# Output projections of a two-layer encoder: one matmul of 512 columns for both halves of the activations

## The chip, the cores and the metric

The kernel runs on one core of one Trainium2 chip. The metric is the device time of one execution in microseconds (us); lower is better. Engines are named as the profile names them: PE is TensorE's matmuls and PEld its weight loads, DVE is VectorE, ACT is ScalarE, POOL is GpSimd, SP is SyncE, which here issues the weight loads from DRAM. ACTq rows are DMAs that ScalarE issues.

## What is computed

The reference is an encoder of 2 layers on 256 tokens of 1024 features, in float32. Each layer is a feed-forward half step, a token mixer, and a second feed-forward half step, all added to the residual x:

```python
x = x + 0.5 * swiglu(rms_norm(x, norm_ffn1[l]), ffn1_in[l], ffn1_out[l])
h = rms_norm(x, norm_mix[l])
proj = h @ w_in[l]
p_rwkv, p_attn, p_gate = jnp.split(proj, [C_RWKV, C_RWKV + C_ATTN], axis=-1)
...
y = jnp.einsum('bsgc,gcd->bsgd', branches, w_branch[l])
merged = jnp.sum(gates * y, axis=2)
x = x + merged @ w_out[l]
x = x + 0.5 * swiglu(rms_norm(x, norm_ffn2[l]), ffn2_in[l], ffn2_out[l])
```

`swiglu` multiplies by a weight matrix of 1024 x 5632 on the way in and by one of 2816 x 1024 on the way out. The mixer runs a bidirectional RWKV-7 scan (branch A) and a differential attention (branch B) side by side; `w_out` is 1024 x 1024.

## The kernel before

Activations lie feature-major: features in the 128 partitions, then the feature tile, then the 256 tokens. Weights stream from DRAM once, in pieces of 128 x 1024 (`weights`, L129 to L140): SP loads `wr`, ACT rounds it to float32r as `wh` (L135), DVE subtracts to get the low part `wl` (L139). `wr` and `wh` have 3 buffers each, `wl` has 2. Activations are split in the same way into a high and a low part. A product of two split operands is three matmuls (`mm3`, L142 to L147): high weights by high part, high weights by low part, low weights by high part. Each has a stationary operand of 128 x 128 and 256 moving columns, the tokens, and all add into one PSUM accumulator `acc`, of which there are 3, each a bank of 512 float32 per partition.

A feed-forward half (`ffn`, L186 to L216) first makes 22 tiles of hidden features, then 8 tiles of output: for each output tile 22 groups of three matmuls, of which the hidden tiles' parts are the moving operands (`hh` and `hl`, six slots shared with mixer tiles and printed in the profile under those names: ar, wt, ab, qb). The tile is added to x by one DVE instruction (L215), and `x_ready` (L150 to L166) at once makes the parts for the next stage: the high part on ACT (L158), the low part on DVE (L159), the square on ACT (L165), its sum over the tiles on POOL (L166). `rstd` (L168 to L183) turns that sum into the norm's factor for every token: a PE matmul (L172), DVE (L174), a power on POOL (L176), DVE (L179), a PE matmul (L181) and a copy on ACT into `rs` (L183). The stage that follows scales its results by `rs` on draining, so its matmuls start earlier than `rs` is there.

The mixer (`mix`, L805 to L840) stores x to DRAM (`xd`, L809), computes lambda from four small vectors that it loads (`lambdas`, L613 to L627: the load at L617, a product and a sum on DVE at L620 and L621, an exponential on ACT at L622), projects, scans and attends in the order of a written plan, and ends with the branch projection (`branch`, L734 to L745, merged at L825 to L828), the load of x back from `xd` (L833) and the output projection (L834 to L840), 8 tiles of 8 groups of three matmuls, again with one addition a tile (L839). Gate tiles (`gates`, L722 to L732: a projection, a DVE scaling at L729, a tanh on ACT at L730) are independent work in it. The attention's own projections (L643 to L645) have the weights as the moving operand, 512 columns of float32r.

Each engine runs its instructions in the order of the program. Within a stage a scheduler in the framework fixes that order when the kernel is built, from priorities and its own timeline; the plan, pool sizes and priorities are the same in both kernels.

Of the kernel before, what the change touches and what calls it, by code (L numbers as in the profile page):

```python
# [54 lines left out]
class Trunk:  # L55
# [21 lines left out]
    def slot(self, tag, shape, dt=F32, half=False):  # L77
        """A tile of 8 KB (or 4) in a partition; tiles of one tag follow each other in place."""
        tag, n = PLACE.get(tag, tag), int(np.prod(shape[1:]))
        t = self.sp.tile([P, 1024 if half else 2048], dt, tag=tag, name=self.nm(tag))  # L80
        v = t[:, :n]
        names = "abcd"[:len(shape) - 1]
        if len(names) > 1:
            v = v.rearrange(f"p ({' '.join(names)}) -> p {' '.join(names)}", **dict(zip(names, shape[1:])))
        return v
# [42 lines left out]
    # weights ------------------------------------------------------------------------------------  # L128
# [13 lines left out]
    def mm3(self, out, w, c, xh, xl, first, last):  # L142
        wh, wl = w[0][:, c * P:(c + 1) * P], w[1][:, c * P:(c + 1) * P]
        mm = self.nc.tensor.matmul
        mm(out, wh, xh, start=first, stop=False)  # L145
        mm(out, wh, xl, start=False, stop=False)  # L146
        mm(out, wl, xh, start=False, stop=last)  # L147

    # the residual and its norm ------------------------------------------------------------------
    def x_ready(self, l, g0, k, start, later=0):  # L150
        """Splits gain * x of one feature tile and adds its squares."""
        nc = self.nc
        x, g = self.x[:, k], self.vec[l][:, g0 + k:g0 + k + 1]
        if start:
            self.xh = self.slot("xh", [P, KD, S], F32R)
            self.xl = self.slot("xl", [P, KD, S], F32R)
# [28 lines left out]
    # feed-forward half step ---------------------------------------------------------------------  # L185
    def ffn(self, l, w_in, w_out, nxt):  # L186
        nc = self.nc
        xh, xl = self.xh, self.xl
        self.rstd()
        hh = [self.slot(f"b{i}", [P, 8, S], F32R) for i in range(3)]  # L190
        hl = [self.slot(f"b{i + 3}", [P, 8, S], F32R) for i in range(3)]
        for j in range(KF):
            ps = self.acc()
            for u in range(2):
                w = self.weights(w_in[j, :, u * 1024:(u + 1) * 1024], 1024)
                for k in range(KD):
                    self.mm3(ps[:, u * S:(u + 1) * S], w, k, xh[:, k], xl[:, k], k == 0, k == KD - 1)
# [7 lines left out]
            a, b = hh[j // 8][:, j % 8], hl[j // 8][:, j % 8]  # L205
            nc.scalar.activation(a, h, AF.Copy)
            nc.vector.tensor_tensor(b, h, a.bitcast(F32), ALU.subtract)
        for j in range(KD):
            ps = self.acc()
            for c in range(3):  # L210
                n = min(8, KF - 8 * c)
                w = self.weights(w_out[j, :, c * 1024:c * 1024 + n * P], n * P)
                for k in range(n):
                    self.mm3(ps[:, :S], w, k, hh[c][:, k], hl[c][:, k], c + k == 0, c == 2 and k == n - 1)
            nc.vector.scalar_tensor_tensor(self.x[:, j], ps[:, :S], 0.5, self.x[:, j], ALU.mult, ALU.add)  # L215
            nxt(j)  # L216

    # one tile of x @ W for two feature tiles, in a bank -----------------------------------------
    def project(self, w_in, tiles):
        ps = self.acc()  # L220
        for i, t in enumerate(tiles):
            w = self.weights(w_in[t], 1024)
            for k in range(KD):
                self.mm3(ps[:, i * S:(i + 1) * S], w, k, self.xh[:, k], self.xl[:, k], k == 0, k == KD - 1)
        return ps

    def shifted(self, l, tiles, outs):
        """outs = p + mu * (centred_shift(p) - p) of RWKV column tiles."""
# [25 lines left out]
    # RWKV-7: everything that the scans need -----------------------------------------------------  # L254
    def rwkv_common(self, l):
        """The low-rank parts and the places of what the pairs of heads give."""
# [58 lines left out]
    def rwkv_pair(self, p):  # L315
        """A pair of heads in both directions; the last part of the second direction waits for the next call."""
# [16 lines left out]
    def turn(self, out, a):  # L333
        """out[h] = a[h].T for both halves of the partitions."""
# [25 lines left out]
    def unit_front(self, p, d, st, sig, a2, da):  # L360
# [3 lines left out]
        # 2 * iclr - 1 = tanh of half the logit  # L364
# [32 lines left out]
    def unit_back(self, p, d, st, bw, kw):  # L397
# [26 lines left out]
        if d == 1:  # L424
            # sum over a head of r * r_k * (k of both directions)
# [8 lines left out]
    # (I - A)^-1 of the 32 x 32 diagonal blocks, one in a partition ---------------------------------  # L434
    def invert(self, q):
# [25 lines left out]
        # 16 x 16 blocks, row by row from below: X[i, j:] = G[i, j:] X[j:, j:]  # L461
# [7 lines left out]
        # the block off the diagonal: X01 = X00 G01 X11, with X00 G01 in the place below G's diagonal  # L469
# [19 lines left out]
    def merge_blocks(self, q):  # L489
        """The blocks off the diagonal: T = D + D A D."""  # L490
# [118 lines left out]
    # differential attention -----------------------------------------------------------------------  # L609
# [56 lines left out]
    def attention_core(self, l):  # L666
# [3 lines left out]
        for h in range(4):  # L670
# [17 lines left out]
            # e0 / s0 - lambda * e1 / s1 = (e0 - lambda * s0 / s1 * e1) / s0  # L688
# [32 lines left out]
    # the token mixer ------------------------------------------------------------------------------  # L721
# [199 lines left out]
```

## Time and profile before

| what | value |
|---|---|
| median of 3 runs | 1410.98 us (1410.39 to 1412.33) |
| profiled execution, first to last instruction (span) | 1406.5 us |
| time of the profiled execution around its span | not given by the profile; the median stands 4.5 us above the span |
| mean granted TensorE clock | 0.987 of full speed |
| PE, PEld busy | 1349.9 us (96%), 1285.0 us (91%) |
| DVE, ACT, POOL busy | 940.7 us (67%), 664.8 us (47%), 288.2 us (20%) |
| first feed-forward's additions to x | from 150.93 to 206.61 us |

The stages follow each other in the span: feed-forward, mixer and feed-forward of the first layer, then the same of the second. Matmuls are pipelined: a row's duration is its latency, and the distance from one start to the next is what it takes of the engine. "Idle before" an instruction tells how long its engine waited and for whom.

### The profile page before, as it was taken

To read this page: it belongs to the slowest core of one execution; us is meant where nothing else is said; L and a number is where in the kernel's file an instruction comes from. 1 tells how busy PE (TensorE), PEld (TensorE's weight loads), DVE (VectorE), ACT (ScalarE), POOL (GpSimd) and SP (SyncE) were. 2 spreads that over 40 slices of the span, in tenths; PEclk is the share of its full clock that TensorE was granted. 3 is DMA by queue.
4 is the path that set the end of the run, shared out by engine and by line. 5 is a ranking of instruction groups with operands and counts; after the bars stand their busy time and mean duration, and the time that the engine had idled before them with its cause. 6 is when DMAs were issued, how large, how long until landed. Compare 5 with 4: busy or idle time off the path is not lost.

```text
span 1406.5 us, 30996 instructions
## 1 busy us (share of the span) xinstructions
PE 1349.9 (96%) x12916; PEld 1285.0 (91%) x12916; DVE 940.7 (67%) x1421; ACT 664.8 (47%) x1059; POOL 288.2 (20%) x284
## 2 busy tenths in 40 slices
PE   6999999998989999999999999999988999999999
PEld 6999998877889899999999999988767888999998
DVE  4655557799957766555556655588999577656644
ACT  5444445344444455444444444554543554544432
POOL 3111015445001112111111111154540010211100
PEclk9999999999999999999999999999999999999999
DMA  6555664325333565556655556633352445555564
GB/s 230 182 181 182 180 207 156 99 91 138 108 103 116 191 229 177 185 181 179 181 184 187 183 174 183 218 111 113 93 143 83 114 136 193 175 187 184 183 188 143
DMA packets 90333, 227.60 MB, mean 162 GB/s; under 512 B 29264, under 2 KB 35408, under 8 KB 89680
## 3 DMA queue, kind: packets, MB, share of 16 engines
q1 hardware_dynamic: 78640, 207.16, 47.0%
q10 hardware_dynamic: 11552, 18.46, 3.9%
q8 instruction: 101, 1.65, 0.5%
q14 instruction: 40, 0.33, 0.1%
HBM read 214.05 MB, written 11.53 MB: 160 GB/s over the span
## 4 chain that ended last, share of the span: by engine, by line
PE 80%; DVE 11%; DMA 3%; issue 2%; ACT 2%; POOL 2%; ACTq 0%; SPq 0%; DVEq 0%; POOLq 0%
PE acc L147 23%; PE acc L146 23%; PE acc L145 23%; DVE tv L458 3%; DVE wl L139 3%; DVE lora L459 2%; PE back L331 1%; PE gen L331 1%; PE att L679 1%; PE back L337 1%; PE gen L283 1%; DMA x<-xd 1%; DMA x<-x 1%; DMA f<-g 0%; PE acc L643 0%
## 5 line engine op out<-in xcount | busy, mean ns | idle before, releaser
L135 ACT ACTIVATE wh<-wr 128x1024 fp32r<-128x1024 f32 (+1 forms) x390 | 404.9, 1039 | 414.7 <-PE acc L146 268.6
L139 DVE TENSOR_TENSOR wl<-wr,wh 128x1024 fp32r<-128x1024 f32 (+1 forms) x390 | 475.5, 1219 | 171.0 <-PE acc L147 83.0
L145 PE MATMUL acc<-xh,wh 128*128 128x256 f32 x1904 | 540.2, 286 | 11.8 <-ACT wh L135 11.8
L146 PE MATMUL acc<-xl,wh 128*128 128x256 f32 x1904 | 539.5, 285 | 0.0
L147 PE MATMUL acc<-xh,wl 128*128 128x256 f32 x1904 | 529.9, 286 | 2.4 <-DVE wl L139 2.1
L145 PEld LDWEIGHTS acc<-xh,wh 128*128 128x128 f32 x1904 | 367.0, 193 | 17.3 <-ACT wh L135 12.0
L146 PEld LDWEIGHTS acc<-xl,wh 128*128 128x128 f32 x1904 | 367.0, 193 | 3.2 <-issue 2.5
L147 PEld LDWEIGHTS acc<-xh,wl 128*128 128x128 f32 x1904 | 360.6, 193 | 9.4 <-issue 3.5
L204 POOL TENSOR_TENSOR t<-t,t 128x256 f32<-128x256 f32 x88 | 89.3, 1016 | 403.7 <-ACT t L202 403.7
L145 PE MATMUL acc<-ar,wh 128*128 128x256 f32 x512 | 144.9, 283 | 0.0
L147 PE MATMUL acc<-ar,wl 128*128 128x256 f32 x512 | 144.9, 283 | 0.0
L199 DVE TENSOR_TENSOR t<-acc,rs 128x512 f32<-128x512 f32 x88 | 60.8, 692 | 119.7 <-PE acc L147 114.6
L146 PE MATMUL acc<-wt,wh 128*128 128x256 f32 x384 | 108.9, 284 | 0.0
L145 PEld LDWEIGHTS acc<-ar,wh 128*128 128x128 f32 x512 | 98.3, 192 | 0.0
L147 PEld LDWEIGHTS acc<-ar,wl 128*128 128x128 f32 x512 | 98.3, 192 | 0.0
L145 PE MATMUL acc<-wt,wh 128*128 128x256 f32 x320 | 91.0, 286 | 3.4 <-DVE x L839 2.2
L166 POOL TENSOR_TENSOR vv<-vv,t 128x256 f32<-128x256 f32 x42 | 36.8, 876 | 279.4 <-ACT t L165 271.8
L147 PE MATMUL acc<-wt,wl 128*128 128x256 f32 x320 | 91.5, 286 | 1.3 <-DVE wl L139 1.2
L458 DVE TENSOR_TENSOR tv<-lora 64x8 f32<-64x8 f32 (+10 forms) x88 | 74.9, 852 | 1.9
L146 PEld LDWEIGHTS acc<-wt,wh 128*128 128x128 f32 x384 | 74.4, 194 | 0.0
L146 PE MATMUL acc<-ab,wh 128*128 128x256 f32 x256 | 72.4, 283 | 0.0
L145 PEld LDWEIGHTS acc<-wt,wh 128*128 128x128 f32 x320 | 61.9, 194 | 4.0 <-issue 2.4
(234 smaller groups left out, 1935.1 us busy)
## 6 DMA issues: line engine op xcount, KB each, us to landing
wr<-f1i SPq DMA_DIRECT2D x88, 512.0 KB, 3.7
wr<-f2i SPq DMA_DIRECT2D x88, 512.0 KB, 3.6
wr<-win SPq DMA_DIRECT2D x62, 512.0 KB, 3.6
wr<-f1o SPq DMA_DIRECT2D x32, 512.0 KB, 3.6
wr<-f2o SPq DMA_DIRECT2D x32, 512.0 KB, 3.6
wr<-watt SPq DMA_DIRECT2D x24, 512.0 KB, 3.7
wr<-wbr SPq DMA_DIRECT2D x16, 512.0 KB, 3.6
wr<-wout SPq DMA_DIRECT2D x16, 512.0 KB, 3.4
```

Of the source, the lines that this page charges most:

```text
L135: nc.scalar.activation(wh[:, :n], raw[:, :n], AF.Copy)
L139: nc.vector.tensor_tensor(wl[:, :n], raw[:, :n], wh[:, :n].bitcast(F32), ALU.subtract)
L145: mm(out, wh, xh, start=first, stop=False)
L146: mm(out, wh, xl, start=False, stop=False)
L147: mm(out, wl, xh, start=False, stop=last)
L166: nc.gpsimd.tensor_tensor(self.sq, self.sq, sq, ALU.add)
L199: nc.vector.tensor_tensor(gu, ps.rearrange("p (a b) -> p a b", a=2), self.rs.unsqueeze(1).to_broadcast([P, 2, S]), ALU.mult)
L204: nc.gpsimd.tensor_tensor(h, s, gu[:, 1], ALU.mult)
L283: mm(ps, dw[r, t * P:(t + 1) * P], w2[r], start=True, stop=True)
L331: self.nc.tensor.matmul(out[r], a[r], b[r], start=start, stop=stop)
L458: mul = lambda o, a, b: ops.append(nc.vector.tensor_tensor(o, a, b, ALU.mult).ins)
L459: add = lambda o, a: ops.append(nc.vector.tensor_reduce(o, a, AX.X, ALU.add).ins)
```

## The change

The high and low part of an activation now lie in one tile, so that both can be read as one moving operand of two pieces of 256 columns. In the output projections of both feed-forward halves and of the mixer, `mm3` gives way to `mmw`: one matmul of 512 columns by the high weights, which fills both halves of the accumulator, and one of 256 columns by the low weights into the left half. The two halves are added on draining: `add_x` has two additions in place of one. `mm3` stays for all other products and only takes its operands from the common tile.

```diff
-    def mm3(self, out, w, c, xh, xl, first, last):
+    def mm3(self, out, w, c, x, first, last):
         wh, wl = w[0][:, c * P:(c + 1) * P], w[1][:, c * P:(c + 1) * P]
         mm = self.nc.tensor.matmul
...
+    def mmw(self, out, w, c, x, first, last):
+
+        wh, wl = w[0][:, c * P:(c + 1) * P], w[1][:, c * P:(c + 1) * P]
+        mm = self.nc.tensor.matmul
+        mm(out.rearrange("p (a b) -> p a b", a=2), wh, x, start=first, stop=last, skip_group_check=True)
+        mm(out[:, :S], wl, x[:, 0], start=False, stop=last, skip_group_check=True)
+
+    def add_x(self, j, ps):
+        for u in range(2):
+            self.nc.vector.scalar_tensor_tensor(self.x[:, j], ps[:, u * S:(u + 1) * S], 0.5, self.x[:, j], ALU.mult, ALU.add)
...
-            self.xh = self.slot("xh", [P, KD, S], F32R)
-            self.xl = self.slot("xl", [P, KD, S], F32R)
+            self.xs = self.sp.tile([P, 2, KD, S], F32R, tag="xs", name=self.nm("xs"))
+            self.xh, self.xl = self.xs[:, 0], self.xs[:, 1]
...
-        hh = [self.slot(f"b{i}", [P, 8, S], F32R) for i in range(3)]
-        hl = [self.slot(f"b{i + 3}", [P, 8, S], F32R) for i in range(3)]
+        hs = [self.slot(f"b{i}", [P, 2, 4, S], F32R) for i in range(6)]
...
-                    self.mm3(ps[:, :S], w, k, hh[c][:, k], hl[c][:, k], c + k == 0, c == 2 and k == n - 1)
-            nc.vector.scalar_tensor_tensor(self.x[:, j], ps[:, :S], 0.5, self.x[:, j], ALU.mult, ALU.add)
+                    self.mmw(ps, w, k, hs[2 * c + k // 4][:, :, k % 4], c + k == 0, c == 2 and k == n - 1)
+            self.add_x(j, ps)
...
-        mh, ml = self.slot("wt0", [P, KD, S], F32R), self.slot("wt1", [P, KD, S], F32R)
+        ms = [self.slot(f"wt{i}", [P, 2, 4, S], F32R) for i in range(2)]
...
-                self.mm3(ps[:, :S], w, k, mh[:, k], ml[:, k], k == 0, k == KD - 1)
-            nc.vector.scalar_tensor_tensor(self.x[:, j], ps[:, :S], 0.5, self.x[:, j], ALU.mult, ALU.add)
+                self.mmw(ps, w, k, ms[k // 4][:, :, k % 4], k == 0, k == KD - 1)
+            self.add_x(j, ps)
```

New lines push the later ones down by 10 or 11: L159 becomes L170, L174 L185, L233 L243, L620 L630, and so on. The order of the instructions moves at places that the diff does not show, since the scheduler lays them anew.

TensorE at the end of the first feed-forward's output projection and the start of the mixer (`acc` of the last output tile, then that of the mixer's first), before:

```order
L145 MATMUL acc_2327<-wt_20_167,wh_2390 128x256
L146 MATMUL acc_2327<-qb_170,wh_2390 128x256
L147 MATMUL acc_2327<-wt_20_167,wl_2392 128x256
L147 MATMUL acc_2459<-xh_1775,wl_2464 128x256
L145 MATMUL acc_2459<-xh_1775,wh_2462 128x256
```

and with the change:

```order
L153 MATMUL acc_2178<-qb_169,wh_2225 128x512
L154 MATMUL acc_2178<-qb_169,wl_2227 128x256
L153 MATMUL acc_2178<-qb_169,wh_2225 128x512
L154 MATMUL acc_2178<-qb_169,wl_2227 128x256
L145 MATMUL acc_2289<-xs_1753,wh_2292 128x256
```

A group of three has become a group of two. VectorE at the same place and in the front of the first mixer (`x` is the residual, `xl` and `xs` its parts, `wl` low weights, `lam` lambda, `rs` the norm's factor), before:

```order
L215 SCALAR_TENSOR_TENSOR x_81<-acc_2327,x_81 128x256
L139 TENSOR_TENSOR wl_2494<-wr_2490,wh_2492 128x1024
L159 SCALAR_TENSOR_TENSOR xl_1776<-x_81,vec_82,xh_1775 128x256
L139 TENSOR_TENSOR wl_2534<-wr_2530,wh_2532 128x1024
L174 TENSOR_SCALAR ms_2421<-gen_2418 128x2
L139 TENSOR_TENSOR wl_2608<-wr_2604,wh_2606 128x1024
L179 TENSOR_SCALAR t_337_2425<-ident,rsT_2423 128x128 x2
L139 TENSOR_TENSOR wl_2638<-wr_2634,wh_2636 128x1024
L620 TENSOR_TENSOR t_342_2436<-t_341_2434 128x128
L621 TENSOR_REDUCE lam_2437<-t_342_2436 128x2
L233 TENSOR_TENSOR t_356_2520<-acc_2459,rs_2430 128x2x256
```

and with the change:

```order
L158 SCALAR_TENSOR_TENSOR x_81<-acc_2178,x_81 128x256
L139 TENSOR_TENSOR wl_2324<-wr_2320,wh_2322 128x1024
L158 SCALAR_TENSOR_TENSOR x_81<-acc_2178,x_81 128x256
L170 SCALAR_TENSOR_TENSOR xs_1753<-x_81,vec_82,xs_1753 128x256
L139 TENSOR_TENSOR wl_2364<-wr_2360,wh_2362 128x1024
L185 TENSOR_SCALAR ms_2251<-gen_2248 128x2
L139 TENSOR_TENSOR wl_2438<-wr_2434,wh_2436 128x1024
L190 TENSOR_SCALAR t_335_2255<-ident,rsT_2253 128x128 x2
L630 TENSOR_TENSOR t_340_2266<-t_339_2264 128x128
L139 TENSOR_TENSOR wl_2468<-wr_2464,wh_2466 128x1024
L631 TENSOR_REDUCE lam_2267<-t_340_2266 128x2
```

The second addition stands behind a weight split, and the product for lambda has moved ahead of the last weight split shown. ScalarE in the front of the first mixer, before:

```order
L617 DMA t_341_2434<-lam 128x256
L135 ACTIVATE wh_2780<-wr_2778 128x1024
L183 ACTIVATE rs_2430<-gen_2428 128x256
L622 ACT_TABLE_LOAD
L622 ACTIVATE lam_2437<-lam_2437 128x2
```

and with the change:

```order
L627 DMA t_339_2264<-lam 128x256
L135 ACTIVATE wh_2610<-wr_2608 128x1024
L632 ACT_TABLE_LOAD
L632 ACTIVATE lam_2267<-lam_2267 128x2
L194 ACTIVATE rs_2260<-gen_2258 128x256
```

The copy of the norm's factor has moved behind the exponential of lambda. The second mixer's front is laid in the same way. In the rest of the mixers the order differs as well, in the first much more than in the second.

## Rows read from the trace of the kernel before

**Rows 1.** The page: busy time of the engines, and the chain that ended last.
```profile
PE 1349.9 (96%) x12916; PEld 1285.0 (91%) x12916; DVE 940.7 (67%) x1421; ACT 664.8 (47%) x1059; POOL 288.2 (20%) x284
...
PE 80%; DVE 11%; DMA 3%; issue 2%; ACT 2%; POOL 2%; ACTq 0%; SPq 0%; DVEq 0%; POOLq 0%
```

**Rows 2.** Busy us by stretch: two feed-forward outputs, one mixer output.
```profile
core 0: us, PE busy (x) PEld busy (x) DVE busy (x) ACT busy (x) POOL busy (x), PEclk, DMA share, GB/s
152.00:206.00 54.00, 54.00 (x452) 54.00 (x452) 27.87 (x34) 24.54 (x34) 5.43 (x6) 1.00 0.63 187
1350.00:1402.00 52.00, 52.00 (x435) 52.00 (x435) 23.40 (x25) 17.72 (x18) 0.00 (x0) 1.00 0.61 174
500.00:517.00 17.00, 16.88 (x141) 16.83 (x141) 12.67 (x20) 10.80 (x19) 4.43 (x6) 1.00 0.61 205
```

**Rows 3.** Timeline of PE, feed-forward output: start, duration (us); 37 alike between.
```profile
159.73 0.28 PE L145 MATMUL acc<-ar,wh 128*128 128x256 f32 x1
...
164.29 0.28 PE L147 MATMUL acc<-ar,wl 128*128 128x256 f32 x1
```

**Rows 4.** Timeline of PE, attention's projections: three matmuls and then two between.
```profile
278.41 0.40 PE L643 MATMUL acc<-wh,xh 128*128 128x512 f32 x1
...
279.34 0.62 PE L645 MATMUL acc<-wl,xh 128*128 128x512 f32 x2
279.80 0.39 PE L643 MATMUL acc<-wh,xh 128*128 128x512 f32 x1
...
280.48 0.39 PE L643 MATMUL acc<-wh,xh 128*128 128x512 f32 x1
```

**Rows 5.** Groups by line: count, busy us, mean ns of one, idle before.
```profile
L215 DVE SCALAR_TENSOR_TENSOR x<-acc,x 128x256 f32<-128x256 f32 x32 | 13.6, 425 | 37.7 <-PE acc L147 37.7
...
L839 DVE SCALAR_TENSOR_TENSOR x<-acc,x 128x256 f32<-128x256 f32 x16 | 6.8, 424 | 14.5 <-PE acc L147 10.6 <-DMA x<-xd 3.9
```

**Rows 6.** Timeline of DVE, end of the first feed-forward output.
```profile
206.61 0.42 DVE L215 SCALAR_TENSOR_TENSOR x<-acc,x 128x256 f32<-128x256 f32 x1 [1.12 <-PE acc L147]
206.95 1.22 DVE L139 TENSOR_TENSOR wl<-wr,wh 128x1024 fp32r<-128x1024 f32 x1
208.08 0.48 DVE L159 SCALAR_TENSOR_TENSOR xl<-x,vec,xh 128x256 fp32r<-128x256 f32 x1
```

**Rows 7.** Timeline of ACT, the same place.
```profile
207.07 0.34 ACTq L809 DMA_DIRECT2D xd<-x  x1
207.50 0.49 ACT L158 ACTIVATE xh<-x,vec 128x256 fp32r<-128x256 f32 x1
```

**Rows 8.** Timeline of PE, first reads of the last feature tile's parts.
```profile
208.93 0.28 PE L145 MATMUL acc<-xh,wh 128*128 128x256 f32 x1
209.05 0.28 PE L146 MATMUL acc<-xl,wh 128*128 128x256 f32 x1
```

**Rows 9.** Timeline of DVE, end of the kernel.
```profile
1403.17 0.42 DVE L215 SCALAR_TENSOR_TENSOR x<-acc,x 128x256 f32<-128x256 f32 x1 [4.02 <-PE acc L147]
```

**Rows 10.** Timeline of ACT, front of the first mixer.
```profile
213.65 0.33 ACTq L617 DMA_DIRECT2D t<-lam  x1
...
218.04 0.39 ACT L183 ACTIVATE rs<-gen 128x256 f32<-128x256 f32 x1 [0.69 <-PE gen L181]
...
219.74 0.20 ACT L622 ACTIVATE lam<-lam 128x2 f32<-128x2 f32 x1
```

**Rows 11.** The lambda load, L617: time from issue to landing.
```profile
DMA to landing us min/median/max: 4.8/5.0/5.2
```

**Rows 12.** Timeline of DVE, front of the first mixer.
```profile
218.85 0.29 DVE L620 TENSOR_TENSOR t<-t 128x128 f32<-128x128 f32 x1 [1.88 <-DMA t<-lam]
219.18 0.29 DVE L621 TENSOR_REDUCE lam<-t 128x2 f32<-128x128 f32 x1
219.38 0.68 DVE L233 TENSOR_TENSOR t<-acc,rs 128x512 f32<-128x512 f32 x1
```

**Rows 13.** Timeline of PE, front of the first mixer.
```profile
217.41 0.60 PE L181 MATMUL gen<-t,ones 128*128 128x256 f32 x2
```

**Rows 14.** Busy us by stretch, first mixer; columns as in rows 2.
```profile
218.00:228.00 10.00, 10.00 (x73) 8.62 (x72) 7.37 (x16) 7.56 (x14) 4.76 (x6) 1.00 0.48 159
388.00:398.00 10.00, 8.57 (x70) 7.73 (x71) 7.28 (x11) 4.18 (x5) 0.00 (x0) 0.66 0.58 139
398.00:408.00 10.00, 8.59 (x147) 7.84 (x145) 6.08 (x13) 5.94 (x16) 0.00 (x0) 1.00 0.71 205
```

**Rows 15.** Timeline of ACT: last head's last exponential, then four gate steps.
```profile
445.22 0.49 ACT L686 ACTIVATE f<-f,n 128x256 f32<-128x256 f32 x1
...
446.93 0.40 ACT L730 ACTIVATE gg<-gg 128x256 f32<-128x256 f32 x1
...
460.63 0.42 ACT L730 ACTIVATE gg<-gg 128x256 f32<-128x256 f32 x1 [0.17 <-DVE gg L729]
```

More of the change, by code (lines that the diff above doesn't have):

```diff
@@ L140, in weights @@
         return wh, wl
-    def mm3(self, out, w, c, xh, xl, first, last):
+    def mm3(self, out, w, c, x, first, last):
         wh, wl = w[0][:, c * P:(c + 1) * P], w[1][:, c * P:(c + 1) * P]
         mm = self.nc.tensor.matmul
-        mm(out, wh, xh, start=first, stop=False)
-        mm(out, wh, xl, start=False, stop=False)
-        mm(out, wl, xh, start=False, stop=last)
+        mm(out, wh, x[:, 0], start=first, stop=False)
+        mm(out, wh, x[:, 1], start=False, stop=False)
+        mm(out, wl, x[:, 0], start=False, stop=last)
+    def mmw(self, out, w, c, x, first, last):
[6 more added lines that the diff above has]
+            self.nc.vector.scalar_tensor_tensor(self.x[:, j], ps[:, u * S:(u + 1) * S], 0.5, self.x[:, j], ALU.mult, ALU.add)
     def x_ready(self, l, g0, k, start, later=0):
@@ L187, in ffn @@
         nc = self.nc
-        xh, xl = self.xh, self.xl
+        xs = self.xs
         self.rstd()
-        hh = [self.slot(f"b{i}", [P, 8, S], F32R) for i in range(3)]
-        hl = [self.slot(f"b{i + 3}", [P, 8, S], F32R) for i in range(3)]
+        hs = [self.slot(f"b{i}", [P, 2, 4, S], F32R) for i in range(6)]
         for j in range(KF):
@@ L196, in ffn @@
                 for k in range(KD):
-                    self.mm3(ps[:, u * S:(u + 1) * S], w, k, xh[:, k], xl[:, k], k == 0, k == KD - 1)
+                    self.mm3(ps[:, u * S:(u + 1) * S], w, k, xs[:, :, k], k == 0, k == KD - 1)
             gu = self.t2()
@@ L204, in ffn @@
             nc.gpsimd.tensor_tensor(h, s, gu[:, 1], ALU.mult)
-            a, b = hh[j // 8][:, j % 8], hl[j // 8][:, j % 8]
+            a, b = hs[j // 4][:, 0, j % 4], hs[j // 4][:, 1, j % 4]
             nc.scalar.activation(a, h, AF.Copy)
@@ L223, in project @@
             for k in range(KD):
-                self.mm3(ps[:, i * S:(i + 1) * S], w, k, self.xh[:, k], self.xl[:, k], k == 0, k == KD - 1)
+                self.mm3(ps[:, i * S:(i + 1) * S], w, k, self.xs[:, :, k], k == 0, k == KD - 1)
         return ps
@@ L742, in branch @@
                 for k in range(4):
-                    self.mm3(ps[:, i * S:(i + 1) * S], w, i * 4 + k, o[:, 0, k], o[:, 1, k], k == 0, k == 3)
+                    self.mm3(ps[:, i * S:(i + 1) * S], w, i * 4 + k, o[:, :, k], k == 0, k == 3)
             done(j, ps.rearrange("p (a b) -> p a b", a=2), g)
@@ L820, in mix @@
         self.gate = None
-        mh, ml = self.slot("wt0", [P, KD, S], F32R), self.slot("wt1", [P, KD, S], F32R)
+        ms = [self.slot(f"wt{i}", [P, 2, 4, S], F32R) for i in range(2)]
         def merge_a(j, ps, g):
-            m = slice(2 * j, 2 * j + 2)
+            m, i = slice(2 * j, 2 * j + 2), slice(2 * j % 4, 2 * j % 4 + 2)
+            mh, ml = ms[j // 2][:, 0, i], ms[j // 2][:, 1, i]
             nc.vector.scalar_tensor_tensor(g, g, 1.0, ps, ALU.add, ALU.mult)
             nc.vector.tensor_tensor(g, g, self.mb[:, m], ALU.add)
-            nc.scalar.activation(mh[:, m], g, AF.Copy)
-            nc.vector.tensor_tensor(ml[:, m], g, mh[:, m].bitcast(F32), ALU.subtract)
+            nc.scalar.activation(mh, g, AF.Copy)
+            nc.vector.tensor_tensor(ml, g, mh.bitcast(F32), ALU.subtract)
         for _ in self.branch(l, 0, self.oa, merge_a):
```

## The prediction

> **What bounds the kernel now.** The page first: TensorE's matmul rows cover 96% of the span, and of the chain that ended last 80% lies on TensorE and 11% on VectorE [rows 1]. Those are averages, so I then took the table by stretches. In the output projection of a feed-forward half (the two rows in [rows 2] that are 54 and 52 us long) TensorE is busy for the whole stretch at a granted clock of 1.00 (2.4 GHz), while VectorE is busy for half of it and ScalarE for less. In the mixer's output projection TensorE still leaves only 0.12 us of 17 open. So in the stages that the change edits TensorE alone sets the pace; what is saved there per matmul is saved in time, and VectorE has room. Next the timeline of TensorE in such a stage: the matmuls of 256 columns start at a fixed step. From 159.73 to 164.29 us there are 39 of them, so 38 steps of 4.56 / 38 = 0.120 us [rows 3]. The duration that the profile gives for one (about 0.28 us) is its latency; the step is the price.
>
> The same trace has matmuls of 512 columns in the same number format, in the attention's projections. Four steps from 278.41 to 279.34 are 0.233 us each, three from 279.80 to 280.48 are 0.227 [rows 4].
>
> **What the change removes.** Each group of three matmuls (high weights by high half, high by low, low by high) becomes one of 512 columns and one of 256. A feed-forward output has 8 feature tiles of 22 groups, 176, and there are 4; a mixer output has 8 x 8 = 64, and there are 2: 704 + 128 = 832 matmuls fewer. A pair cost 2 x 0.120 = 0.240 us. For the wide one I take 0.227: the stretch with that step is the one that has wide matmuls alone and no slower neighbour, and it leaves 0.227 - 0.120 = 0.107 us for 256 more columns, so 0.013 us of every matmul that does not depend on its columns. Saved: 832 x 0.013 = **10.8 us**. Upper bound of the step: 0.240, two pieces of 256 at the old price, since the moving operand is now two pieces that lie apart, a form that this trace doesn't show; then nothing is saved. The lower bound is the 0.227 itself, the fastest step seen.
>
> What a page states here differs. By the Trainium skill, "TensorE: Matmul & The Clock Gate", section "Back-to-back issue gap", a warm matmul takes N / 2.4 + 2.5 ns, so one matmul less would save 2.5 ns, by this page an estimate of 832 x 2.5 ns = 2.1 us. The rows do not bear that out: they leave 13 ns beyond 256 / 2.4 at either width.
>
> **What it adds, covered.** Each of the 48 feature tiles is now drained by two VectorE additions instead of one, each some 0.425 us [rows 5]. Inside a stage this costs nothing: VectorE's half-idle time covers it, and three accumulator banks let TensorE run on. Without that cover it would be 48 x 0.43 = 20 us. The weight loads move no more bytes, and arrive at 187 GB/s in these stages; a stage shorter by 4% asks for 194, and 205 is seen in the mixer's output [rows 2].
>
> **What it adds, uncovered: the stage ends.** The next stage reads the last residual tile. Before, at the first feed-forward's end: addition at 206.61, a weight split until 208.17, the low half of x from 208.08 [rows 6], the high half on ScalarE from 207.50 [rows 7]. TensorE's first reads of the two are at 208.93 and 209.05 [rows 8]: 0.5 us after the low half's end at 208.56. Now VectorE's order is addition, weight split, second addition, low half. So the second addition starts at 208.08, ends at about 208.5; the high half then ends at 209.04 and the low half at about 209.6. TensorE waits 209.6 - 209.05 = 0.55 us. Three such ends (feed-forward to mixer twice, feed-forward to feed-forward once): 1.65. At the two ends of the mixer's output another split of x (0.4 us) stands between as well: about 1.0 each, 2.0. At the kernel's end the second addition stands before the store, 1403.17 being the last one now [rows 9]: 0.43. Sum **4.1 us**; bounds 0.4 (the last alone, if TensorE's first reads slip behind other matmuls) and 6.5 (no slack at any of the five: the low half is 209.6 - 208.56 = 1.04 later at three ends and 1.45 at two, and the 0.43).
>
> **What it moves.** The program's order in the mixers is written by a scheduler, and shifts. At the front of both mixers one thing changes that can be priced. VectorE's product of the lambda vectors (L620, now L630) waits for a small load; it stood behind the weight split of the first receptance tile, and now stands ahead of it. In the trace the load is issued at 213.65 [rows 10], such a load takes 4.8 to 5.2 us [rows 11], and VectorE begins the product at 218.85 after 1.9 us of waiting for it [rows 12]. Queued behind the product now: that weight split (0.3 + 1.2 us, so done at 220.4), and behind ScalarE's exponential of lambda also the copy of the norm's factor, which ran at 218.04, before it [rows 10]. Who waits: TensorE, whose matmul for that factor was at 217.41 [rows 13] and now stands five matmuls earlier, reaches the first product with the late weights some 13 matmuls after it, at about 218.8, with the wait at the stage's end 219.35. It stands for 220.4 - 219.35 = 1.05 us. The store of x into DRAM (207.07 [rows 7]) also goes out 1.5 us later, behind the second addition, and shares the DMA engines with the weights ahead of the lambda load, so the load can be up to 1.5 later: 2.5 us. The first drain of the mixer (219.38 [rows 12]) is later by 2.0 with the load on time: split until 220.4, then the reduction, the exponential and the copy (0.29 + 0.20 + 0.39) until 221.3. Bounds 0 and 2.5 per mixer; I take 1.4, nearer the row: **2.8 us** for two.
>
> Elsewhere the second mixer's order is nearly the old one. The first mixer's is shuffled in many places; I cost that at nothing and leave it to a rival (rival 2).
>
> **Sum.** -10.8 + 4.1 + 2.8 = -3.9 us. The span of 1406.5 becomes 1402.6. The median of the runs shown stands 4.5 us above the span, and I carry that over: **1407.1 us**. About 0.2%, 2.8 us, is what a measurement of this kernel can tell from no change: faster means below 1408.2, slower above 1413.8.
>
> **Rivals.**
> 1. *The mixers swallow the wait.* After the front TensorE has idle time, for example 1.4 us in each of the stretches from 388 to 408 [rows 14], where a late start can be made up. For it: those stretches wait on VectorE's and the scan's work, not on TensorE. Against: the product chain starts 2 us late too, and right behind the front, from 218 to 228, TensorE is full. Then -10.8 + 4.1 = -6.7: 1404.3.
> 2. *The first mixer loses cover.* The gate tiles (24 x 0.12 = 2.9 us of TensorE each) fill the time in which the last attention head's softmax runs. Before, four of the gates' ScalarE steps come after that head's last exponential [rows 15]; now two do in the first mixer, four still in the second. If what was covered comes to light, 2 x 2.9 = 5.8 us: -3.9 + 5.8 = +1.9, 1412.9. For it: nothing else independent is left at that place. Against: the two tiles are then done earlier, in idle time that rows 14 show.
> 3. *The wide matmul is hardly cheaper than two: slower.* The place is every group of the six output stages; the price is the step of 512 columns. The added 6.9 us eat the gain when the step is 0.240 - 6.9 / 832 = 0.2317 us, and the slower stretch of [rows 4], 0.233, is already beyond that. With it the gain is 832 x 0.0075 = 6.2, the result +0.7: 1411.7; with 0.240 it is +6.9: 1417.9. For it: the two-piece operand. Against: a steady 0.227 where nothing disturbs, and a stage with no other load on TensorE. The page's formula above belongs here: by its 2.5 ns the result would be 1411.0 - 2.1 + 6.9 = 1415.8. That the change doesn't do what it says would be this case with 0.240.
>
> **How the numbers follow.** Forecast 0.50, its own range 1404 to 1410 (wait 0 to 2.5 per mixer, ends 2 to 6.5); rival 1 0.22; rival 2 0.18; rival 3 0.10. Range: downwards 10.8 with 0.4 of added time, 1400.6, so 1400; upwards rival 2 with 2 us more, 1415; left out are most of rival 3 and the tails. Faster: two thirds of the forecast and all of rival 1, 0.56; same: the rest of the forecast but little, over half of rival 2, 0.27; slower: the rest, 0.17.
>
> **What would show it.** Step right: wide matmuls starting 0.227 apart from what follows, additions of one feed-forward output 22 x 0.347 = 7.63 us apart instead of 7.92. Ends: TensorE waiting 0.5 to 1.0 us for the low half of x. Front: VectorE waiting over 3 us for the lambda load, TensorE then over 1 us for the weight split. Wrong, if the additions stay 7.9 us apart (rival 3), if the two mixers differ from their old lengths by more than 4 us, or if TensorE idles over 4 us ahead of the branch projection (rival 2).

## The result and the profile after

The changed kernel takes **1420.22 us** (median of 4 runs, 1419.25 to 1422.65); the kernel before, beside it, 1410.68 us (1410.28 to 1412.33). The ratio is 1.0067, with a 95% interval of 1.0053 to 1.0082: slower by some 9.5 us, where the prediction had 3.9 us faster and a range that ended at 1415. Its profiled execution has a span of 1417.4 us.

First the page, busy time and the chain that ended last, to be held against [rows 1]:

```profile
PE 1350.6 (95%) x12084; PEld 1245.5 (88%) x12084; DVE 961.8 (68%) x1469; ACT 665.9 (47%) x1059; POOL 302.8 (21%) x284
...
PE 75%; DVE 14%; DMA 5%; POOL 2%; issue 2%; ACT 2%; SPq 0%; ACTq 0%; DVEq 0%; POOLq 0%
```

832 matmuls are gone, as counted. TensorE's share of the chain fell from 80 to 75%, VectorE's rose from 11 to 14% and that of DMA from 3 to 5%: what was saved on TensorE came back as waiting. Next the stages that were edited. Timeline of PE in the first feed-forward's output (start, duration), beside [rows 3]; 25 matmuls stand between:

```profile
159.73 0.40 PE L153 MATMUL acc<-ar,wh 128*128 128x512 f32 x1
...
164.24 0.39 PE L153 MATMUL acc<-ab,wh 128*128 128x512 f32 x1
```

Thirteen groups of a wide and a narrow matmul take 4.51 us, 0.347 a group: with 0.120 for the narrow one the wide one costs 0.227. Timeline of DVE in that stage, the two additions of one feature tile and the first of the next, and then its end and the front of the first mixer, beside [rows 6, 12]:

```profile
151.50 0.42 DVE L158 SCALAR_TENSOR_TENSOR x<-acc,x 128x256 f32<-128x256 f32 x1 [1.07 <-PE acc L154]
152.97 0.42 DVE L158 SCALAR_TENSOR_TENSOR x<-acc,x 128x256 f32<-128x256 f32 x1
158.90 0.42 DVE L158 SCALAR_TENSOR_TENSOR x<-acc,x 128x256 f32<-128x256 f32 x1 [0.80 <-PE acc L154]
...
204.80 0.42 DVE L158 SCALAR_TENSOR_TENSOR x<-acc,x 128x256 f32<-128x256 f32 x1 [0.80 <-PE acc L154]
205.14 1.22 DVE L139 TENSOR_TENSOR wl<-wr,wh 128x1024 fp32r<-128x1024 f32 x1
206.27 0.42 DVE L158 SCALAR_TENSOR_TENSOR x<-acc,x 128x256 f32<-128x256 f32 x1
207.27 0.48 DVE L170 SCALAR_TENSOR_TENSOR xs<-x,vec,xs 128x256 fp32r<-128x256 f32 x1 [0.58 <-ACT xs L169]
...
218.33 0.29 DVE L630 TENSOR_TENSOR t<-t 128x128 f32<-128x128 f32 x1 [5.00 <-DMA t<-lam]
```

The step from one feature tile to the next alternates between 7.4 and 7.9 us; from 151.50 to 204.80 it is 53.30 / 7 = 7.61 (forecast 7.63, before 7.92). The order at the stage's end is the one forecast: addition, weight split, second addition, low half. Timeline of PE there, beside [rows 8]; the middle row is the first read of the low half:

```profile
207.34 0.33 PE L145 MATMUL acc<-xs,wh 128*128 128x256 f32 x1
207.81 0.38 PE L146 MATMUL acc<-xs,wh 128*128 128x256 f32 x1
208.03 0.28 PE L147 MATMUL acc<-xs,wl 128*128 128x256 f32 x1
```

The two steps are 0.47 and 0.22 us where 0.12 is usual, so 0.45 us is lost (forecast 0.55). At the front VectorE waits 5.00 us for the lambda load (before 1.88, [rows 12]), and TensorE for the split behind it:

```profile
219.81 0.39 PE L147 MATMUL acc<-xs,wl 128*128 128x256 f32 x1 [2.02 <-DVE wl L139]
```

So all that was priced is there, at about its price. In this one profile the granted clock of the stretch around that wait was 0.83, where it was 1.00 before [rows 14]; that was not priced. Busy us by stretch of the changed kernel, columns as in [rows 2]:

```profile
218.00:228.00 10.00, 8.19 (x46) 7.36 (x47) 7.79 (x15) 5.31 (x11) 3.74 (x5) 0.83 0.40 133
```

The main part of what was not priced stands at the other end of the first mixer. Timeline of ACT there, beside [rows 15]: the last head's last exponential, and the gate steps that follow it.

```profile
459.84 0.49 ACT L696 ACTIVATE f<-f,n 128x256 f32<-128x256 f32 x1
...
463.99 0.42 ACT L740 ACTIVATE gg<-gg 128x256 f32<-128x256 f32 x1 [2.61 <-DVE gg L739]
...
467.84 0.41 ACT L740 ACTIVATE gg<-gg 128x256 f32<-128x256 f32 x1
```

The exponential ends 14.6 us later than in the kernel before, though the mixer began 0.3 us earlier, and two gate steps are left to follow it instead of four. Timeline of PE from there to the branch projection, the three longest gaps (7.05 us), and then two of the five of the kernel before (2.15 us in all):

```profile
464.80 0.68 PE L347 MATMUL gen<-ident,t 64*64 64x64 f32 x16 [2.51 <-DVE t L600]
473.24 0.63 PE L726 MATMUL att<-ident,osb 128*128 128x128 f32 x4 [2.93 <-ACT t L608]
475.47 1.12 PE L726 MATMUL att<-ident,osb 128*128 128x128 f32 x4 [1.61 <-DVE icl L729]
```

```profile
460.40 0.63 PE L716 MATMUL att<-ident,osb 128*128 128x128 f32 x4 [0.54 <-DVE osb L713]
...
465.37 0.62 PE L145 MATMUL acc<-icl,wh 128*128 128x256 f32 x3 [0.78 <-ACT icl L718]
```

TensorE stands idle for over 7 us behind the last head where it stood for about 2. And then its clock falls. Busy us by stretch of the changed kernel, columns as in [rows 2]:

```profile
147.00:205.00 58.00, 58.00 (x336) 50.72 (x336) 35.42 (x46) 27.79 (x37) 7.31 (x6) 1.00 0.64 192
...
511.00:528.00 17.00, 16.39 (x93) 14.24 (x94) 16.19 (x25) 10.79 (x18) 5.77 (x5) 1.00 0.62 219
...
465.00:475.00 10.00, 5.93 (x112) 5.04 (x108) 8.12 (x21) 5.58 (x13) 2.48 (x3) 0.95 0.50 159
475.00:485.00 10.00, 9.23 (x68) 8.71 (x69) 4.94 (x10) 2.17 (x3) 0.91 (x1) 0.71 0.11 25
```

From 475 to 485 TensorE is busy again, at a granted clock of 0.71, so part of the time at 1.2 GHz. Measured from the last addition of one stage to the last of the next, the first mixer grew from 310.9 to 324.7 us and the second from 313.1 to 316.3; a feed-forward half fell from 190.94 to 189.31. The gain is there, and in these profiles the first mixer eats it.

How much of the 13.8 us lies behind the last head? Busy us of the 35 us from the start of its last exponential, before and then with the change:

```profile
445.22:480.22 35.00, 32.86 (x372) 31.06 (x371) 25.89 (x54) 16.15 (x31) 4.63 (x5) 0.95 0.47 150
459.84:494.84 35.00, 27.65 (x283) 26.04 (x282) 21.75 (x44) 13.48 (x24) 4.71 (x4) 0.90 0.49 152
```

TensorE's idle time there is 7.35 us against 2.14, and the lower clock costs 35 x 0.05 = 1.75 us of full-speed work more: together 7.0, about half. Nearly all the rest lies ahead of that exponential. The last exponentials of the four heads start 7.7, 9.9, 12.6 and 15.0 us later than before, counted from the feed-forward's end, so most of the lateness is there before the fourth head begins. Lateness is not loss by itself: from the last exponential to the mixer's last addition it is 71.2 us, before 72.3, since work that stood behind it now stands ahead.

### The profile page after: what moved, and what is told of

It reads as the page before. It is cut to its first block, busy times and chain, and to the rows that moved or that the text cites. A ratio compares the mean times of both kernels' runs of the same rounds, so it can differ in the third digit from the quotient of the medians.

```text
span 1417.4 us, 29341 instructions
## 1 busy us (share of the span) xinstructions
PE 1350.6 (95%) x12084; PEld 1245.5 (88%) x12084; DVE 961.8 (68%) x1469; ACT 665.9 (47%) x1059; POOL 302.8 (21%) x284
## 4 chain that ended last, share of the span: by engine, by line
PE 75%; DVE 14%; DMA 5%; POOL 2%; issue 2%; ACT 2%; SPq 0%; ACTq 0%; DVEq 0%; POOLq 0%
PE acc L147 15%; PE acc L146 15%; PE acc L145 15%; PE acc L153 13%; PE acc L154 6%; DVE wl L139 4%; DVE tv L468 3%; DVE lora L469 2%; PE back L341 1%; DMA lora<-d 1%; PE gen L341 1%; PE att L689 1%; DMA g<-gg 1%; PE back L347 1%; PE gen L293 1%
## 5 line engine op out<-in xcount | busy, mean ns | idle before, releaser
L145 PE MATMUL acc<-xs,wh 128*128 128x256 f32 x1904 | 542.3, 287 | 13.0 <-ACT wh L135 12.3
L146 PE MATMUL acc<-xs,wh 128*128 128x256 f32 x1904 | 542.1, 287 | 0.7
L147 PE MATMUL acc<-xs,wl 128*128 128x256 f32 x1904 | 532.0, 287 | 5.1 <-DVE wl L139 5.1
L145 PEld LDWEIGHTS acc<-xs,wh 128*128 128x128 f32 x1904 | 368.9, 194 | 19.9 <-ACT wh L135 12.5
L146 PEld LDWEIGHTS acc<-xs,wh 128*128 128x128 f32 x1904 | 369.0, 194 | 4.8 <-DVE xs L170 2.1
L147 PEld LDWEIGHTS acc<-xs,wl 128*128 128x128 f32 x1904 | 362.3, 194 | 11.7 <-DVE wl L139 6.0
L153 PE MATMUL acc<-wt,wh 128*128 128x512 f32 x384 | 137.0, 398 | 1.4 <-DVE f L836 1.3
L153 PE MATMUL acc<-ar,wh 128*128 128x512 f32 x256 | 91.3, 394 | 0.0
L153 PEld LDWEIGHTS acc<-wt,wh 128*128 128x128 f32 x384 | 72.7, 190 | 18.7 <-ACT wh L135 2.0
L154 PEld LDWEIGHTS acc<-wt,wl 128*128 128x128 f32 x384 | 73.2, 191 | 5.3 <-DVE wl L139 5.2
L154 PE MATMUL acc<-ar,wl 128*128 128x256 f32 x256 | 71.3, 279 | 0.0
L153 PEld LDWEIGHTS acc<-ar,wh 128*128 128x128 f32 x256 | 48.1, 188 | 9.9
```

The lines of the kernel that those rows point to most:

```text
L145: mm(out, wh, x[:, 0], start=first, stop=False)
L146: mm(out, wh, x[:, 1], start=False, stop=False)
L147: mm(out, wl, x[:, 0], start=False, stop=last)
L153: mm(out.rearrange("p (a b) -> p a b", a=2), wh, x, start=first, stop=last, skip_group_check=True)
L154: mm(out[:, :S], wl, x[:, 0], start=False, stop=last, skip_group_check=True)
```

## The experiments

The theory is that the new order in the first mixer costs the time; the rival, that the edit itself does, with its additions, its stage ends and its late x. Times below are medians, each with its ratio to the kernel before on the same chip, and its interval. The medians of the kernel before are 1408.9 to 1410.2 there, with single runs from 1402 to 1419 us, so the intervals reach 2 to 4 us either way, and one profile shows where, not how much: e1 and e15 are one program, and the second mixer takes 324 us in the profile of the one and 314 in that of the other.

### Order or edit: e1, e15, e2

To hold an order, every instruction of a mixer up to its output projection is queued behind the one that stands ahead of it in a table (ORDER); this sets the order on an engine and adds no wait for a result. The tables are the orders of the two kernels. Holding by itself costs nothing that shows: e8 below, held in the changed kernel's own order and with an earlier load, takes 1418.85 us, the changed kernel 1420.22.

```diff
+    def pin(self, l, before):
...
+        for e, runs in ORDER.get(str(l), {}).items():
+            mine = [i for i in traced if str(i.engine).endswith("." + e)]
+            seq = [mine[a + k] for a, n in runs for k in range(n)]
+            for a, b in zip(seq, seq[1:]):
+                self.tc.add_manual_dep(b, a.name, mybir.DependencyInfo(
+                    mybir.DependencyClass.NoSync, mybir.DependencyReason.DATA), reason="pin")
...
         nc.scalar.dma_start(self.x, xd)
+        self.pin(l, before)
```

> The changed kernel, with the instructions of both mixers (up to the output projection) held on every engine in the order that the kernel before has. Theory A, the new order in the mixers costs the time: what is left is 832 matmuls at 0.013 us less, -10.8 us, and the stage ends, +4.1, so about 1404 us, 16 less than the changed kernel. Theory B, the change itself costs it (two additions for one, the stage ends, the late start of the mixer): the order does little, 1416 to 1420 us. Theory C, wide matmuls save nothing: 1414 us or more, with 7.9 us between feed-forward outputs.

> The run with the old order once more, beside the two above on one chip: 0.9968 of the kernel before, again within the interval 0.9946 to 0.9990.

> The kernel before, nothing wide, with both mixers held in the order of the changed kernel on every engine. Theory A (order): slower than the kernel before by what the mixers lost in the changed kernel, 12.9 + 2.3 us less what lies in the first mixer's late start, so 1421 to 1426 us. Theory B (the change itself): 1410 to 1413 us.

e1: 1404.67 us, 0.9968 (0.9946 to 0.9990). e15: 1404.96 us, 0.9961 (0.9940 to 0.9982). e2: 1418.72 us, 1.0059 (1.0040 to 1.0078). The edit without its new order is faster than the kernel before by 5 us, as theory A has it, and the new order without the edit is slower by 8, with not one wide matmul in it. That is less than theory A's 1421 to 1426, so its amount is a miss, but clear of theory B's 1410 to 1413. Theory C falls, and theory B as the whole cause. The two effects don't add up: -5 and +8 make +3, and the changed kernel has +9.5. Some 6 us, give or take 4, come only when edit and order stand together; what makes them was not tested.

### What the edit costs by itself: e7

The old order is held, and the wide matmul is issued as two narrow ones into the two halves of the accumulator. This kernel serves for its time alone: it keeps two accumulations open in one bank at a time and leaves the right sums out.

```diff
-        mm(out.rearrange("p (a b) -> p a b", a=2), wh, x, start=first, stop=last, skip_group_check=True)
+        mm(out[:, :S], wh, x[:, 0], start=first, stop=False, skip_group_check=True)
+        mm(out[:, S:], wh, x[:, 1], start=first, stop=last, skip_group_check=True)
```

> The old order in both mixers, two accumulator halves and two additions as in the changed kernel, but each wide matmul is issued as two of 256 columns: what is added without what is saved. If the additions and the stage ends cost the 4.1 us of the prediction: 1414 to 1415. If the saving is larger and they cost more than that: the difference to the run with the old order and wide matmuls is the saving, 10.8 us by the step of 0.013 us; if they cost nothing: 1410.

1414.30 us, 1.0039 (1.0026 to 1.0053): 5.5 us over the kernel before, where the prediction had 4.1 for the stage ends. Against e1 the wide matmul gives back 0.0071 x 1410 = 10.0 us; the prediction had 10.8. The stages are sharper than the totals: the feed-forwards between two additions take 190.94 us before, 191.60 with halves (+0.66 a stage end, forecast 0.55) and 189.31 with wide matmuls, 2.29 less, which is 176 x 0.013.

### Front, early or late part: e3, e4, e5, e6, e8

Only the tables differ, each put together from the two orders.

```diff
-ORDER: both mixers as before
+ORDER: as in the changed kernel at the fronts (e3); behind the first mixer's front (e4);
+       there, up to the attention core (e5); there, from the core on (e6)
```

> The changed kernel; in both mixers only the front (the lambda product ahead of the first receptance tile's weight split, with the factor of the norm behind it) keeps the new order, all behind it stands as in the kernel before. Theory A1, the front costs its own wait alone, 1.4 to 2.5 us a mixer: 3 to 5 us over the run with the old order, so 1407 to 1409. Theory A2, the late front sets the whole of the first mixer back: 1414 to 1420. If the mixers swallow the wait: as with the old order, 1404.

> The changed kernel; the front of both mixers and all of the second stand as in the kernel before, only what follows the front of the first mixer keeps the new order. Theory A1, the middle of the first mixer costs some 10 us by itself (its attention core is 14 us late there): 10 us over the run with the old order, about 1414. Theory A2, the front is the cause: as with the old order, about 1404.

> The changed kernel with the old order, except one stretch of the first mixer: from behind the front to the first instruction of the attention core (last head pair, attention projections, first inversion) stands the new order. Theory E, the loss comes early, where VectorE is full and the second inversion is set back: 8 to 12 us over the run with the old order, 1413 to 1417. Theory L, it comes from the attention core on, where the gate tiles now stand ahead of the heads: 0 to 3 us over it, 1404 to 1408.

> The changed kernel with the old order up to the first instruction of the first mixer's attention core, and the new order of the first mixer from there on; the second mixer is old. Theory E: 0 to 4 us over the run with the old order, 1404 to 1409. Theory L: most of the 13 us that the whole middle costs, 1412 to 1418.

e3: 1408.00 us, 0.9987 (0.9966 to 1.0008). e4: 1417.53 us, 1.0054 (1.0028 to 1.0080). e5: 1411.88 us, 1.0022 (1.0005 to 1.0039). e6: 1420.69 us, 1.0072 (1.0045 to 1.0099). The middle costs 12 us over e1 and the front 2.7 with an interval that takes in zero. Either part of the middle costs something alone, the early one 7.6 us, the late one 14.7. The two don't add up to e4, so each may have an effect of its seam in it, the place where one order passes into the other; that was not tested. What I take from them is that either part alone suffices for a loss, the late one for most of it. In e3's trace the lambda load went out earlier in the first mixer than in the changed kernel, so it tests the second front more than the first.

For the front by itself, the lambda vectors of both layers are loaded once at the kernel's start, in the changed kernel's own order.

```diff
+        self.lamv = [self.cp.tile([P, 4, 64], F32, name=f"lamv{l}") for l in range(L)]
...
-        lv = self.t1().rearrange("p (a b) -> p a b", a=4)
-        nc.scalar.dma_start(lv, self.io["lam"][l:l + 1].to_broadcast([P, 4, 64]))
+        lv = self.lamv[l]
```

> The changed kernel in its own order in both mixers; the lambda vectors of both layers are loaded once at the kernel's start, so that the lambda product waits for no load. If the lambda wait at the fronts costs its 1.4 us and more a mixer: 3 to 5 us less than the changed kernel, 1415 to 1417. If the mixers swallow it: 1420. If the late front is what sets the first mixer back: 1406 to 1410.

1418.85 us, 1.0074 (1.0050 to 1.0099): no gain that these runs can tell, though in its profile the norm's factor comes 2.4 us earlier. What a front costs, between nothing and some 3 us, stays open.

### Where in the attention core: e9, e13

The new order of the first mixer begins later: behind the second head (e9) or behind the third (e13).

```diff
-ORDER: first mixer new from the attention core on (e6)
+ORDER: first mixer new from the third head on (e9), from the fourth head on (e13)
```

> As the run with the new late part, but the first mixer keeps the old order longer, to where the blocks of the second inversion are merged: heads 0 and 1 of the attention are then done in the old order, and the new order holds for heads 2 and 3, the second chain and the last gate tiles. Theory H, the loss is made at the core's entry, where VectorE stands idle behind a gate tile's product that it was queued for too early: at most 5 us over the run with the old order, 1405 to 1410. Theory G, it is made at the end, where too few gate tiles are left to cover the last head: 10 to 15 us over it, 1415 to 1420.

> The changed kernel with the old order; in the first mixer the new order begins only behind the third head of the attention core, so the fourth head, the rest of the second chain and the last gate tiles alone stand in it. Theory Q, each head loses time by itself, because its score matmuls, its VectorE steps and its ScalarE copies stand behind a gate tile or the scan in the new order: the loss over the old order alone goes on falling, 14.7 from the core's entry, 8.5 from the third head, here 0 to 5 us. Theory G, the loss is made at the end, where too few gate tiles are left to cover the last head: it stays at 8 us or more.

e9: 1411.78 us, 1.0028 (1.0011 to 1.0046), 0.0060 x 1410 = 8.5 us over e1, between the two theories, so a miss for both. e13: 1412.75 us, 1.0020 (1.0002 to 1.0038), 0.0059 x 1410 = 8.3 us over e15. The amount is that of theory G: what comes from the fourth head on carries 8 us by itself, though with an interval of 4 to 12 us, which does not shut out the 5 us of theory Q. In the profiles both ways are seen. Timelines of e15, old order: PE, the fourth head's two pairs of score matmuls; ACT, its last exponential and the first gate steps behind it:

```profile
436.19 1.13 PE L696 MATMUL att<-icl 64*128 64x256 f32 x4
440.89 1.13 PE L696 MATMUL att<-icl 64*128 64x256 f32 x4
...
445.20 0.49 ACT L703 ACTIVATE f<-f,n 128x256 f32<-128x256 f32 x1
446.90 0.40 ACT L747 ACTIVATE gg<-gg 128x256 f32<-128x256 f32 x1
451.36 0.42 ACT L747 ACTIVATE gg<-gg 128x256 f32<-128x256 f32 x1 [1.52 <-DVE gg L746]
```

The same of e13, with the VectorE instruction that takes the scores:

```profile
443.15 0.28 PE L154 MATMUL acc<-xs,wl 128*128 128x256 f32 x1
...
444.61 1.13 PE L696 MATMUL att<-icl 64*128 64x256 f32 x4
449.43 1.13 PE L696 MATMUL att<-icl 64*128 64x256 f32 x4
...
445.77 0.69 DVE L697 SCALAR_TENSOR_TENSOR f<-att,dist 128x512 f32<-128x512 f32 x1 [3.39 <-PE att L696]
...
455.94 0.49 ACT L703 ACTIVATE f<-f,n 128x256 f32<-128x256 f32 x1
459.01 0.42 ACT L747 ACTIVATE gg<-gg 128x256 f32<-128x256 f32 x1 [1.53 <-DVE gg L746]
```

Measured from the feed-forward's end, both mixers are equally far at the third head's exponentials, to within 0.7 us. In e13 matmuls of gate tiles (the last of them before the first pair is the first row, at 443.15) and steps of the scan stand ahead of the scores on TensorE, VectorE waits 3.39 us for the scores, and the head's softmax ends 10.7 us later. In part this is e13's seam: what the new order has ahead of the third head and the old one behind it stands here all at once ahead of the fourth. Between the last exponentials of the two heads TensorE has 517 matmul rows in e13, 399 in e15 and 394 in the changed kernel, which comes to its 15.0 us by degrees, from the first head on. Then the PE rows with idle time of e13 up to the branch projection:

```profile
459.83 0.68 PE L354 MATMUL gen<-ident,t 64*64 64x64 f32 x16 [1.44 <-DVE t L607]
468.26 0.63 PE L733 MATMUL att<-ident,osb 128*128 128x128 f32 x4 [2.93 <-ACT t L615]
470.87 1.12 PE L733 MATMUL att<-ident,osb 128*128 128x128 f32 x4 [1.98 <-DVE icl L736]
```

Busy us by stretch of e13, columns as in [rows 2]:

```profile
460.00:470.00 10.00, 5.96 (x112) 5.06 (x110) 7.90 (x20) 5.58 (x13) 2.45 (x3) 1.00 0.47 161
470.00:480.00 10.00, 9.13 (x63) 8.69 (x64) 5.17 (x10) 2.19 (x4) 0.94 (x1) 0.66 0.07 15
```

and the stretch of e15 that corresponds:

```profile
460.00:470.00 10.00, 8.02 (x91) 7.07 (x92) 7.46 (x19) 4.23 (x9) 2.60 (x3) 1.00 0.46 157
```

The idle time is 6.35 us against 2.1, so 4.2 more; and the stretch behind runs at 0.66 of the clock, 3.4 us of full-speed work less. Together 7.6 of the 8.3 measured. What repeats in every profile is the idle time: in the 35 us from the start of the last exponential TensorE is idle for 5.1 to 7.4 us in all seven profiles with the new late order, and for 2.0 to 2.4 us in all ten with the old one. Ahead of that exponential the two sets overlap (13.4 to 16.6 and 11.5 to 16.3 us), so where the early loss is made stays open. The sum takes the low clock as the idle time's due: the mean granted clock from 255 to 275 us behind the feed-forward's end is 0.83 or less in the profiles of all kernels with the new late order, and 0.91 or more in all with the old one. No run set the clock by itself.

### Attempts at a better version: e10, e11, e14, e12

e10 moves the weight split behind the low half of x at five stage ends; e11 has also the early lambda load; e14 leaves the last feature tile of each output narrow, so that one addition ends the stage. All three hold the old order. e12 holds nothing: the changed kernel with the early lambda load alone.

```diff
-            g = self.gate() if self.gate else None
+            g = self.gate() if self.gate else self.last_split if self.nw == 1 else None
...
+        if j == KD - 1:
+            return self.mm3(out[:, :S], w, c, x, first, last)
...
-        for u in range(2):
+        for u in range(1 if j == KD - 1 else 2):
```

> Old order and wide matmuls, and at the five stage ends that another stage follows the second weight split of the next stage stands behind the low half of the last residual tile on VectorE, no longer ahead of the second addition. If the stage ends cost what the stage lengths say (0.66 us a feed-forward, about 1 at the others), 3 to 4 us less than the old order alone: about 1401. If TensorE then waits for the weight split instead: no change, 1404 to 1405.

> As the run before it, and the lambda vectors loaded once at the kernel's start. If the lambda product's load still costs something at the two fronts in the old order: 1 to 3 us less, 1398 to 1400. If not: the same time within 1 us.

> Old order; in each of the six output stages the last feature tile goes back to three matmuls of 256 columns and one addition, the other seven stay wide. The stage ends are then those of the kernel before, at the price of 22 (or 8) x 0.013 = 0.29 (or 0.10) us each. If the stage ends cost 0.66 us a feed-forward and about 1 at the others: 2 to 3 us less than the old order alone, a feed-forward stage 0.3 to 0.4 us shorter. If they cost nothing: 1.4 us more.

> The changed kernel with nothing held, the scheduler free, and the lambda vectors loaded once at the kernel's start. The order that comes out is nearly the old one in the second mixer and much nearer to it in the first (414 rows of TensorE's differ there, against 1438). If the loss grows with how far the first mixer's attention core is set back behind gate tiles: between the run with the old order and the changed kernel, 1404 to 1412. If any departure from the old order costs the whole: 1417 to 1420.

e10: 1406.06 us, 0.9986 (0.9968 to 1.0003): a miss. A feed-forward takes 189.80 us instead of 189.31; in its profile TensorE then waits 0.39 us for the weight split at the first feed-forward's end, and 0.67 us for POOL's sum of the squares at the second's. Ahead of the second addition was the better place. e11: 1407.69 us, 0.9981 (0.9965 to 0.9997), the same. e14: **1400.25 us, 0.9928** (0.9901 to 0.9955, 6 runs), which is faster than both kernels; but its feed-forwards take 189.51 and 189.86 us, not the 0.3 to 0.4 less that was expected, and its interval overlaps that of e15, so that the narrow last tile is better than the old order alone is not shown. In its profile the mixers are the shorter ones, 311.3 and 311.0 us against 313.5 and 314.0 in that of e15. e12: 1407.51 us, 1.0006 (0.9982 to 1.0029): between, as expected of an order near the old one, though its interval takes in the kernel before. In its profile the last head ends as early as in the kernel before.

## Why the prediction was wrong, point by point

- **The wide matmul, -10.8 us: right.** The step is 0.227, a feed-forward's additions 7.61 us apart, and e7 against e1 gives 10.0. By the Trainium skill, "TensorE: Matmul & The Clock Gate", section "Back-to-back issue gap", an isolated warm matmul costs 2.5 ns beyond its columns, which makes an estimate of 2.1 us for 832 of them; the feed-forwards' 2.29 us for 176 matmuls, 13 ns each, decide against using that price for this stream of float32r matmuls. With them rival 3 falls.
- **Additions inside a stage, nothing: right** in the feed-forwards, where VectorE is busy for 35 of 58 us. In the mixer's output VectorE is busy for 16.2 of 17 and TensorE idle for 0.61, where it was 0.12 [rows 2], so there the cover is all but used up.
- **Stage ends, +4.1: right.** TensorE loses 0.45 us at the first feed-forward's end, and all that is added comes to 5.5 (3.7 to 7.5) by e7, an interval that holds the 4.1.
- **The fronts, +2.8: the waits came as told** (5.00 us for the load, TensorE 2.02 for the split, where 1.05 was worked out with the load on time). What they cost in the end is too little for e3, e8 and e11 to show. The forecast's own range, 1404 to 1410, is narrower than the bounds it names: waits of 0 to 5.0 and ends of 2 to 6.5 us give 1402 to 1412.
- **The step that failed:** "The first mixer's is shuffled in many places; I cost that at nothing and leave it to a rival". In the changed kernel it cost 0.0102 x 1410 = 14 us with the fronts, from e1 and e15 to the changed kernel, more than the 10 us that the wide matmul gave; in the kernel before, by e2, it cost 8. Two of the prediction's signs of being wrong were there: the first mixer grew by over 4 us, and TensorE stood idle for over 4 us ahead of the branch projection.
- **Rival 2 had the sign, and the place of about half of it.** Two gate steps stand behind the last exponential instead of four, and TensorE is idle for 5.2 us more behind it, close to the 5.8 that the rival was priced at. It missed two things. With that idle time goes a lower granted clock, which takes another 1.75 us in the changed kernel and 3.4 in e13. And the first mixer loses as much again ahead of the last head, where e5 shows that the early part of the new order costs 7.6 us alone; by which step is open. The argument against the rival, that the tiles are then done earlier in idle time, fails: TensorE's idle time ahead of the last exponential did not shrink (16.6 us, before 13.4), and in e13 such matmuls stand in front of the scores, which wait.
- **Rival 1**, 1404.3, is the time of the old order (1404.7 and 1405.0), but it got there by an order that the changed kernel does not have; that the numbers agree is chance.

## What to carry to other kernels

Where a scheduler writes the order, a change that saves 0.013 us a matmul can reshuffle a stage that it does not touch; compare the order on every engine, and price what moved ahead of the longest chain, not only what the edit adds. Look first at fillers that moved ahead of the next step of that chain on the engine that runs both: here two gate tiles done early left a hole behind the last head. If the order is the cost, hold the old one and measure the edit alone, before the edit is given up.

## What the runs showed of the hardware

- A matmul of 512 float32r columns whose moving operand is two pieces of 256 that lie apart steps by 0.227 us, like one with its columns in one piece ([rows 4]).
- The gaps behind the last head came with a lower clock: around and behind 6.35 and 7.05 us of gaps on TensorE (e13 and the changed kernel) the granted clock of 10 us was 0.66 and 0.71, so part of the time at 1.2 GHz. Medians of the mean clock over a whole execution were 0.979 to 0.982 for the kernels with the new late order and 0.984 to 0.987 for those with the old order throughout, but 0.981 also for e5, whose late order is the old one.
